# Modulation units emitted two by two in the first phase of a hybrid decoder step, with a fifth weight buffer

## The chip, the core and the metric

The kernel runs on one core of a Trainium2 chip. The metric is the device time of one execution in microseconds. The core has five engines that matter here: TensorE (PE, its weight loads PEld), VectorE (DVE), ScalarE (ACT), GpSimd (POOL) and SyncE (SP), whose queue issues nearly all DMA transfers, in order.

## What is computed

One inference step of a decoder layer with three token mixers, for 256 prompt tokens and 8 x 4 sample tokens, 288 rows in all. What matters here is how the layer begins: nine condition vectors (one for the prompt, eight for the samples) go through one large product, whose result modulates the normalised input, and the modulated input goes through the input projection.

```
def _layer(x, c, w_ada, b_ada, g_norm, w_in, ...):
    m = jax.nn.silu(c) @ w_ada + b_ada
    shift, scale, gate = jnp.split(m[:, None, :], 3, axis=-1)
    h = _rmsnorm(x, g_norm) * (1 + scale) + shift
    (u_a, v_a, z_a, qkv_b, z_b, a_b, b_b, q_c, k_c, v_c, z_c, qi_c, ki_c, wi_c) = _split_in(h @ w_in)
    ...
    mix = jnp.concatenate([y_a, y_b, y_c], axis=-1)
    x = x + gate * (mix @ w_out)
```

The model width is 4096, `w_ada` is 4096 x 12288, `w_in` 4096 x 14960, and all numbers are 32 bits wide. The mixers themselves, the final norm and the cache outputs come later in the kernel and are not touched.

## The kernel before

**Dense products.** A weight tile `w` holds 2 x 128 rows and 512 columns (512 KB). It is loaded by SyncE into one of `N_RAW` = 4 buffers and split, 128 rows at a time, into a high part `wh` (a cast on ACT) and the rest `wl` (a subtraction on DVE), with `N_SPLIT` = 4 buffers each. h is split in the same way into `hH` and `hL`. For each 128 columns and 128 rows there are three products of 288 columns (`wh` with `hH`, `wh` with `hL`, `wl` with `hH`), which add up in one of four accumulators `acc0` to `acc3`, each with one buffer. One `w` tile is thus 2 x 4 x 3 = 24 products.

**Modulation units.** The class `Ada` is one unit: two tiles `wa` of 128 x 1024 (512 KB each), and four small products of 32 x 512 that stand on four column groups of TensorE at once; since each is carried out in two passes, the trace shows eight records. The nine condition vectors are the fixed operand, padded to 32. Enough units after each other give shift and scale for 256 or 512 features, from which `make_h` builds h for these features.

**The first phase.** It is cut into 11 stages by features of h (`STEPS`: six stages of 256 features, then five of 512). In each stage the features' part of 12 column groups is computed: a narrow group `c` of 112 columns first, then eleven groups of 512. Each group ends with an addition on DVE (a copy on ACT in the first stage) that evicts the accumulators. The units of a stage must be done before its dense products. Stage 0 has 8 units, which run alone at the start. The other 120 are spread over the dense work of the stages before theirs.

**What sets the order.** The list of all units, dense and modulation, is made once, by the loop at line 899. `rate` is units per dense unit so that each later stage's units are done `LEAD` units ahead, and

```
            e = min(len(la), n0 + int(rate * (j + 1)) // PAIR * PAIR)
            W.units += [u] + la[n:e]
```

puts into the list as many modulation units as `rate` has made due, rounded down to a multiple of `PAIR`. Loads are then issued in the order of this list by `prefetch` as far as buffers are free: `w` into `N_RAW`, `wa` into `N_ADA`. All go through SyncE's queue, so a load that waits for its buffer holds up all that stand behind it. A `wa` buffer is free when the unit that read it is done. At the end of the first phase the pools are exchanged, and a second phase (attention, delta rule, further dense groups, output projection) runs with units of its own, which load into `w` buffers and are governed by other constants.

Of the kernel before, what the change touches and what calls it, by code (L numbers as in the profile page):

```python
# [36 lines left out]

GCOL = [512 * i for i in range(22)] + [C_QC + 512 * i for i in range(7)]
FULL = [(0, 128), (128, 128), (256, 128), (384, 128)]
N_RAW, N_ADA, N_SPLIT = 4, 4, 4  # L40
N_BANK = 4
HOP = 0.22
LEAD = 5
BACKLOG = 2.0
CALM = 2.5
NH = 3
LEAD0 = 0
GMO = 12
PAIR = 1
GATE = 8  # L50
GATE0 = 0
GPAIR = 1
# [328 lines left out]
def tile_hybrid_step(ctx: ExitStack, tc: tile.TileContext, I, O):  # L381
# [517 lines left out]
    while i < len(lb):  # L899
        rate, nxt = max([((min(len(la), la_end[j] + LEAD) - n) / (at_[j] - at_[i]), j) for j in range(i + 1, len(lb))],  # L900
                        default=(0, len(lb)))
        us = [u for x in lb[i:nxt] for u in x]
        n0 = n
        for j, u in enumerate(us):
            e = min(len(la), n0 + int(rate * (j + 1)) // PAIR * PAIR)
            W.units += [u] + la[n:e]
# [1576 lines left out]
```

## Time and profile before

| | |
|---|---|
| runs | 2639.38, 2645.76, 2648.55 us; median 2645.76 |
| profiled execution | 2644.57 us, span 2642.8 us |
| mean granted TensorE clock | 0.986 |
| busy | PE 96%, PEld 85%, DVE 62%, ACT 40%, POOL 19% |
| HBM | 587.54 MB read, 24.95 MB written |

The span runs from the first to the last instruction of the program; the execution's own time has 1.8 us around it. A busy share is the time in which an engine had at least one instruction under way. All durations below are from the profiled execution.

### The profile page before, as it was taken

The page shows a single profiled execution, that of the slowest core. Times are in us where ns is not written, and L with a number is a line of the kernel's source. Part 1 is how long each engine was busy: PE and PEld are TensorE (multiplying, and loading weights), DVE is VectorE, ACT ScalarE, POOL GpSimd, SP SyncE. Part 2 cuts the span into 40 slices and gives each one's busy share as a digit, 9 for nine tenths or more (in the row PEclk, how much of TensorE's full clock was granted, in tenths as well). Part 3 has the DMA queues.
Part 4 walks back from the last instruction along what each step waited for, and adds up shares of the span by engine and source line. Part 5 has one row for each costly group of instructions (what it writes and reads, how often), then busy time and mean ns, then how long its engine had stood idle before and what let it go on. Part 6 is the DMA issues. An engine that isn't in the chain of part 4 may idle for free.

```text
span 2642.8 us, 52171 instructions
## 1 busy us (share of the span) xinstructions
PE 2531.5 (96%) x19684; PEld 2237.9 (85%) x19684; DVE 1629.5 (62%) x3633; ACT 1064.3 (40%) x2440; POOL 495.5 (19%) x1137
## 2 busy tenths in 40 slices
PE   5999999999998999999999989999999999999997
PEld 2777878888897878877789969989989989999997
DVE  3377765555567777744457658568576667555554
ACT  3433233323244443334254444444444544444443
POOL 1000000000001042263542333443440210000000
PEclk9999999999999999999999999999999999999998
DMA  7998988888656477677767547567568465655564
GB/s 276 339 326 327 346 320 301 313 312 302 239 171 209 162 236 239 207 278 251 255 221 248 173 147 245 179 212 255 178 202 267 146 193 183 179 181 177 175 187 164
DMA packets 234964, 615.91 MB, mean 233 GB/s; under 512 B 38856, under 2 KB 92348, under 8 KB 234712
## 3 DMA queue, kind: packets, MB, share of 16 engines
q1 hardware_dynamic: 223672, 574.65, 64.6%
q0 software_dynamic: 11040, 37.92, 4.2%
q8 instruction: 155, 2.54, 0.4%
q14 instruction: 97, 0.79, 0.1%
HBM read 587.54 MB, written 24.95 MB: 232 GB/s over the span
## 4 chain that ended last, share of the span: by engine, by line
PE 85%; DMA 6%; DVE 3%; issue 2%; POOL 2%; ACT 1%; SPq 0%; another core or an unknown queue 0%; ACTq 0%; DVEq 0%; POOLq 0%
PE acc L74 68%; PE ada L74 7%; DMA kraw<-in_cache_k_dram,ixk 2%; DMA wa<-in_w_ada_t_dram 1%; PE Sup L74 1%; PE kT L74 1%; PE YP L74 1%; DVE wl L74 1%; DMA w<-in_w_in_t_dram 1%; PE v L74 1%; PE so L74 1%; PE gram L74 1%; PE o L74 1%; DMA prev<-in_state_conv_dram 0%; DMA vraw<-in_cache_v_dram,ixv 0%
## 5 line engine op out<-in xcount | busy, mean ns | idle before, releaser
L74 DVE TENSOR_TENSOR wl<-w,wh 128x512 fp32r<-128x512 f32 (+1 forms) x1216 | 803.0, 682 | 694.9 <-ACT wh L74 645.1
L74 ACT CAST wh<-w 128x512 fp32r<-128x512 f32 (+1 forms) x1216 | 714.3, 611 | 1173.3 <-PE acc L74 846.0
L74 PE MATMUL acc<-hH,wh 128*128 128x288 f32 (+1 forms) x3744 | 1159.7, 310 | 14.4 <-ACT hH L74 8.7
L74 PE MATMUL acc<-hH,wl 128*128 128x288 f32 (+1 forms) x3744 | 1108.7, 296 | 6.0 <-DVE wl L74 3.9
L74 PE MATMUL acc<-hL,wh 128*128 128x288 f32 (+1 forms) x3744 | 1107.8, 296 | 1.3 <-issue 0.9
L74 PEld LDWEIGHTS acc<-hH,wh 128*128 128x128 f32 (+1 forms) x3744 | 706.4, 189 | 175.6 <-ACT wh L74 90.2
L74 PEld LDWEIGHTS acc<-hH,wl 128*128 128x128 f32 (+1 forms) x3744 | 706.9, 189 | 9.7 <-DVE wl L74 7.6
L74 PEld LDWEIGHTS acc<-hL,wh 128*128 128x128 f32 (+1 forms) x3744 | 707.4, 189 | 4.4 <-issue 3.2
L74 PE MATMUL acc<-mL,wh 128*128 128x288 f32 x1024 | 302.4, 295 | 2.5 <-DVE mL L74 2.5
L74 PE MATMUL acc<-mH,wh 128*128 128x288 f32 x1024 | 304.3, 297 | 0.0
L74 PE MATMUL acc<-mH,wl 128*128 128x288 f32 x1024 | 302.8, 296 | 0.0
L74 PEld LDWEIGHTS acc<-mL,wh 128*128 128x128 f32 x1024 | 193.0, 188 | 2.7 <-DVE mL L74 2.7
L74 PEld LDWEIGHTS acc<-mH,wh 128*128 128x128 f32 x1024 | 192.9, 188 | 0.2
L74 PEld LDWEIGHTS acc<-mH,wl 128*128 128x128 f32 x1024 | 192.9, 188 | 0.0
L74 PE MATMUL ada<-wa,cT 128*32 128x512 f32 x1024 | 149.9, 619 | 17.6 <-DMA wa<-in_w_ada_t_dram 17.6
L74 DVE TENSOR_TENSOR zb<-zb,acc 128x288 f32<-128x288 f32 x160 | 70.6, 451 | 41.1 <-PE acc L74 40.4
L74 POOL TENSOR_TENSOR htmp<-yT,gaT 128x32 f32<-128x32 f32 x20 | 7.7, 387 | 449.9 <-DVE gaT L74 449.9
L74 POOL TENSOR_SCALAR frs<-frs 128x1 f32<-128x1 f32 (+1 forms) x3 | 0.9, 296 | 451.2 <-DVE frs L74 451.1
L74 POOL TENSOR_SCALAR tap<-xp,cwT 128x32 f32<-128x32 f32 x144 | 79.5, 552 | 0.1
L74 DVE TENSOR_TENSOR R<-R,R 128x248 f32<-128x248 f32 (+30 forms) x248 | 72.5, 292 | 10.8 <-DMA w<-in_w_in_t_dram 2.2
L74 DVE SCALAR_TENSOR_TENSOR cv<-xp,cwT,cv 128x256 f32<-128x256 f32 x144 | 70.3, 488 | 3.7
L74 POOL DMA_INDIRECT vraw<-in_cache_v_dram,ixv x64 | 65.2, 1019 | 31.2 <-issue 14.7
(462 smaller groups left out, 2350.5 us busy)
## 6 DMA issues: line engine op xcount, KB each, us to landing
w<-in_w_in_t_dram SPq DMA_DIRECT2D x464, 512.0 KB
wa<-in_w_ada_t_dram SPq DMA_DIRECT2D x256, 512.0 KB
w<-in_w_ada_t_dram SPq DMA_DIRECT2D x128, 512.0 KB
w<-in_w_out_t_dram SPq DMA_DIRECT2D x128, 512.0 KB
St<-in_state_dn_dram SPq DMA_DIRECT2D x16, 512.0 KB
out_dram<-St SPq DMA_DIRECT2D x16, 512.0 KB
X<-in_x_prompt_dram SPq DMA_DIRECT2D x8, 512.0 KB
XF<-in_x_prompt_dram SPq DMA_DIRECT2D x16, 256.0 KB
```

The source lines that it names most:

```text
L74: r = f(*a, **k)
```

## The change

Three constants.

```
-N_RAW, N_ADA, N_SPLIT = 4, 4, 4
+N_RAW, N_ADA, N_SPLIT = 4, 5, 4
 N_BANK = 4
 HOP = 0.22
-LEAD = 5
+LEAD = 6
...
-PAIR = 1
+PAIR = 2
```

With `PAIR` = 2 the modulation units come two at a time, `LEAD` = 6 makes the spread end one unit further ahead of each stage, and there are five `wa` buffers. No instruction is added or removed.

The first place is TensorE's queue at the start of the second stage, where the narrow group is followed by the first wide one. `ada` is the accumulator of the modulation units (x4 is one unit), `acc` with 112 columns the narrow group, with 128 a wide one. Before:

```order
L74 MATMUL ada<-wa,cT 32x512 x4
L74 MATMUL acc_1160<-hH_479,wh 112x288
L74 MATMUL acc_1160<-hL_491,wh 112x288
L74 MATMUL acc_1160<-hH_479,wl 112x288
L74 MATMUL acc_1160<-hH_479,wh 112x288
L74 MATMUL acc_1160<-hL_491,wh 112x288
L74 MATMUL acc_1160<-hH_479,wl 112x288
L74 MATMUL ada<-wa,cT 32x512 x4
L74 MATMUL acc_1178<-hH_479,wh 128x288
```

The same place after:

```order
L74 MATMUL ada<-wa,cT 32x512 x8
L74 MATMUL acc_1164<-hH_483,wh 112x288
L74 MATMUL acc_1164<-hL_495,wh 112x288
L74 MATMUL acc_1164<-hH_483,wl 112x288
L74 MATMUL acc_1164<-hH_483,wh 112x288
L74 MATMUL acc_1164<-hL_495,wh 112x288
L74 MATMUL acc_1164<-hH_483,wl 112x288
L74 MATMUL acc_1180<-hH_483,wh 128x288
```

Two units now stand together ahead of the narrow group, and none is left between it and the wide one. Of the eleven narrow groups six are followed at once by a unit in before and two after; the four that are no longer so are those of the first, second, sixth and tenth stage.

The second place is SyncE's queue in the second stage. `wa` are tiles of modulation units, `w` of dense products. Before:

```order
L74 DMA wa_1314<-in_w_ada_t_dram 128x1024
L74 DMA wa_1316<-in_w_ada_t_dram 128x1024
L74 DMA w_1318<-in_w_in_t_dram 128x1024
L74 DMA wa_1381<-in_w_ada_t_dram 128x1024
L74 DMA wa_1383<-in_w_ada_t_dram 128x1024
L74 DMA w_1389<-in_w_in_t_dram 128x1024
```

After:

```order
L74 DMA wa_1162<-in_w_ada_t_dram 128x1024
L74 DMA wa_1224<-in_w_ada_t_dram 128x1024
L74 DMA wa_1226<-in_w_ada_t_dram 128x1024
L74 DMA wa_1232<-in_w_ada_t_dram 128x1024
L74 DMA w_1234<-in_w_in_t_dram 128x1024
L74 DMA w_1236<-in_w_in_t_dram 128x1024
L74 DMA w_1256<-in_w_in_t_dram 128x1024
L74 DMA wa_1258<-in_w_ada_t_dram 128x1024
L74 DMA wa_1395<-in_w_ada_t_dram 128x1024
```

The four `wa` tiles of a pair now stand together, and two or three `w` tiles behind them. The first of the four (`wa_1162`, then `wa_1258`) has the fifth buffer and can go out ahead of the others, which stand in the queue until the pair before has run and freed their buffers. Between two pairs there are two blocks of 24 products, but a single one twice in the first stage; from the second to the sixth stage two and three in turn, up to the ninth three, and then four or five.

## Rows read from the trace of the kernel before

**Rows 1.** The page: busy time by engine; chain that ended last, by engine.

```profile
PE 2531.5 (96%) x19684; PEld 2237.9 (85%) x19684; DVE 1629.5 (62%) x3633; ACT 1064.3 (40%) x2440; POOL 495.5 (19%) x1137
...
PE 85%; DMA 6%; DVE 3%; issue 2%; POOL 2%; ACT 1%; SPq 0%; another core or an unknown queue 0%; ACTq 0%; DVEq 0%; POOLq 0%
```

**Rows 2.** Five stretches: busy by engine (PE to POOL), granted clock, DMA share, GB/s.

```profile
0.00:56.50 56.50, 28.17 (x150) 12.10 (x150) 19.33 (x46) 20.73 (x39) 13.15 (x36) 0.97 0.83 296
56.50:114.60 58.10, 56.92 (x379) 40.80 (x379) 17.67 (x33) 30.27 (x73) 1.88 (x8) 0.95 0.85 305
114.60:720.20 605.60, 602.71 (x4396) 491.26 (x4392) 377.80 (x792) 183.53 (x335) 19.86 (x64) 1.00 0.86 313
720.20:803.00 82.80, 76.76 (x548) 74.95 (x548) 58.30 (x123) 36.26 (x71) 2.38 (x9) 0.94 0.56 176
803.00:2642.80 1839.80, 1766.98 (x14221) 1618.80 (x14219) 1156.40 (x2639) 793.50 (x1925) 458.19 (x1020) 0.99 0.64 205
```

**Rows 3.** Waits of PE in the third stretch: us in total, times, longest.

```profile
PE acc L74 <- DVE v_c L74: 2.1, 4, 0.6
PE acc L74 <- ACT wh L74: 0.6, 1, 0.6
```

**Rows 4.** A stretch in which DMA is full, columns as in rows 2.

```profile
120.00:128.00 8.00, 8.00 (x55) 6.33 (x55) 4.95 (x12) 2.17 (x4) 0.00 (x0) 1.00 1.02 407
```

**Rows 5.** Timeline of PE around one lone unit: start, duration, operation.

```profile
299.82 0.29 PE L74 MATMUL acc<-hH,wl 128*128 128x288 f32 x1
300.04 1.07 PE L74 MATMUL ada<-wa,cT 128*32 128x512 f32 x8
301.04 0.40 PE L74 MATMUL acc<-hH,wh 128*128 128x288 f32 x1
301.28 0.30 PE L74 MATMUL acc<-hL,wh 128*128 128x288 f32 x1
...
304.20 0.29 PE L74 MATMUL acc<-hH,wl 128*128 128x288 f32 x1
```

**Rows 6.** Records of the units' products: ns min/median/max, first and last start.

```profile
L74 PE MATMUL ada<-wa,cT x1024: 592/616/1063, 20.0 to 720.7; 128*32 128x512 f32 x171
```

**Rows 7.** Timeline of PE at the start, units alone, idle time before in brackets.

```profile
20.02 3.11 PE L74 MATMUL ada<-wa,cT 128*32 128x512 f32 x8 [12.08 <-DMA wa<-in_w_ada_t_dram]
...
32.05 1.05 PE L74 MATMUL ada<-wa,cT 128*32 128x512 f32 x4 [0.34 <-DMA wa<-in_w_ada_t_dram]
...
42.39 4.87 PE L74 MATMUL ada<-wa,cT 128*32 128x512 f32 x16 [3.24 <-DMA wa<-in_w_ada_t_dram]
```

**Rows 8.** The chain that ended last, at the start: start, us, what.

```profile
26.01 6.00 DMA wa<-in_w_ada_t_dram
...
35.67 6.67 DMA wa<-in_w_ada_t_dram
```

**Rows 9.** The same chain in the first stage.

```profile
80.47 6.09 DMA wa<-in_w_ada_t_dram
...
86.61 1.05 PE ada L74 x4
```

**Rows 10.** Timeline of SyncE's issues behind the unit of rows 5.

```profile
301.14 0.81 SPq L74 DMA_DIRECT2D wa<-in_w_ada_t_dram  x2
```

**Rows 11.** Timeline of PE: end of a narrow group, no unit behind.

```profile
165.72 0.29 PE L74 MATMUL acc<-hH,wl 128*112 128x288 f32 x1
166.64 0.37 PE L74 MATMUL acc<-hH,wh 128*128 128x288 f32 x1 [0.64 <-DVE v_c L74]
```

**Rows 12.** Timeline of PE behind the first stage, units alone.

```profile
115.55 2.12 PE L74 MATMUL ada<-wa,cT 128*32 128x512 f32 x8
...
121.00 1.87 PE L74 MATMUL ada<-wa,cT 128*32 128x512 f32 x8
```

**Rows 13.** Timeline of PE: the last stage's first product.

```profile
727.10 0.58 PE L74 MATMUL acc<-hH,wh 128*112 128x288 f32 x1 [4.48 <-ACT hH L74]
```

**Rows 14.** Waits of ScalarE in the third stretch: us, times, longest.

```profile
ACT wh L74 <- DMA w<-in_w_in_t_dram: 103.1, 32, 5.4
```

## Prediction

> **What bounds the kernel now.** I read the page first, then the run cut into five stretches, then the waits inside the third of them, then single instructions. The page says that TensorE is busy for 96% of the span and that 85% of the chain that ended last is TensorE's own work [rows 1]. The five stretches [rows 2] are: up to the first dense product (56.5 us), the first stage with 13 interleaved modulation units (58.1 us), the stages with the other 107 (605.6 us), the last stage without units (82.8 us), and all that comes after (1839.8 us). The edit changes the first three alone: behind the last unit both programs have the same order. In the third stretch TensorE is busy for 602.7 of 605.6 us, and its waits there come to 2.7 us [rows 2, 3]. So time is saved there by giving TensorE less to do, and lost by making it wait. DMA moves 313 GB/s there at a share of 0.86; where it is full it moves 407 [rows 2, 4], which is 1.29 us for a 512 KB tile (524,288 B / 407 GB/s).
>
> **What a unit costs TensorE.** In a run of dense products one starts every 0.133 us (22 steps from 301.28 to 304.20) [rows 5]. Around a lone unit it goes: last product 299.82, unit 300.04, next product 301.04, the one after it 301.28. Two steps of 0.133 would do for what took 1.46, so the unit costs 1.19 us. Of this 0.09 is lost on entry (0.22 for 0.133), 0.11 on the second product after it (0.24 for 0.133), and some of the 1.00 in the middle on the way out. How much, I take from the unit's inside: its eight records are two passes on each of four column groups. One record lasts a median of 0.616 us by the profile's model [rows 6] and the unit 1.07 from first start to last end [rows 5], so the second pass starts 0.45 after the first; half a unit, two column groups alone, takes the same 1.05 [rows 7]. So passes follow each other at 0.45, and a unit that follows a unit would cost two of them, 0.906, in place of 1.19. **Each merge of two lone units saves 0.286 us.** No trace of before has two units back to back with their tiles there, so this is an estimate, between 0.09 (the entry alone is saved) and 0.33 (a pass takes 0.43). I take 0.286, since the pace of passes shows in every unit.
> The Trainium skill, TensorEngine Tiling (Array Packing), Key Properties, says that a change of tiling mode drains TensorE; its page TensorE: Matmul & The Clock Gate, Single matmul latency, puts the constant that a warm stream hides at 166 ns. Two of these a merge would be 0.33 us, and the merges below 17.9 us in place of 15.4; the row decides for the smaller.
>
> **The terms, in order of time.**
> *Start, -4.0.* The first 16 tiles come at the pace of release: the first unit starts at 20.02 and the last half unit at 46.2 (the run that starts at 42.39 lasts 4.87, its last half 1.05) [rows 7], 1.75 us a tile. The chain runs through tiles that were asked for only when a buffer came free (6.00 and 6.67 us) [rows 8]. Four tiles in a round trip of 7.0 us become five, 1.40 a tile; for the 11 tiles after the first five that is 3.9. What follows is a fixed chain (transposes, modulated h, first product) and moves with it. Bounds: 0, and 11 x (1.75 - 1.29) = 5.1.
> *First stage, +1.8.* A block is the 24 products of one w tile, 24 x 0.133 = 3.19 us. Ideal for before: 11 blocks + 0.8 for the narrow group + 13 x 1.19 = 51.4. It took 58.1: 6.7 lost, 2.9 of it at the lower clock (0.95 granted means a tenth of the stretch at 1.2 GHz) [rows 2], so 3.8 in waits, as on the tile of 6.09 us [rows 9]. After the change 14 units stand there in 7 pairs: 14 x 1.19 - 7 x 0.286 = 14.7 for 15.5, so -0.8. But two of the pairs follow the one before after a single block. A first tile lands 5.2 to 6.7 us after its issue (6.67 for one; 6.00 and 6.09 for two second tiles, which were issued 0.43 later and land 1.29 later) [rows 8 to 10]. SyncE issues 1.10 after a unit's start (301.14 against 300.04) [rows 5, 10]. So the last of the three tiles that a pair still needs lands at 1.10 + 5.2 + 2 x 1.29 = 8.9 from the start of the pair before. With one block between, it is used at 3.19 + 2.10 + 0.91 = 6.2: 2.7 late, twice, +5.4. The 3.8 of old waits go: with two blocks between, tiles are in time (below). And the unit between the first narrow group and the next covered a copy and a split of weights, of which about 1 us is now waited for. -0.8 + 5.4 - 3.8 + 1.0 = +1.8. Bounds -3 and +4.
> *One unit earlier, -1.2.* The first stage holds 14 units for 13, the later stretch 106 for 107.
> *Merges, -15.4.* 107 lone units become 53 pairs: 54 switches fewer, x 0.286. Bounds -4.9 and -17.8.
> *Narrow groups, +2.4.* After each stage's 112-column group the next group needs the same accumulator, which DVE must have evicted. A bare wait costs 0.64 idle, 0.79 in all (165.72 to 166.64 for a step of 0.13) [rows 11]; four of these make up the 2.1 us of the third stretch [rows 3]. A unit in between covers it. By the order of after, three later stages lose that cover: 3 x 0.79.
> *Late tiles, +3.6.* From the second to the sixth stage pairs follow each other after two and three blocks in turn. Two blocks: next pair at 2 x 3.19 + 2.10 = 8.5, its second unit at 9.4; its last tile lands at 8.9 with 5.2, at 10.4 with 6.7. I take 0.3 for each of 12 such gaps. With three blocks it is used at 12.6, never late. The w tiles issued behind them land from 10.2 on and are first used at 13.8, so 3.6 us cover ScalarE's and DVE's split of some 1.3; without that cover each gap would wait for it. Bounds 0 and 12 x 1.0 = 12.
> By the Trainium skill, DMA: Bandwidth & Descriptors, Anatomy of one DMA, a lone 512 KB transfer takes 2.0 + 524288/436e3 = 3.2 us (a fit made on GpSimd's path). By it no tile would be late after two blocks and the sum would be 3.6 lower; the transfers of these rows took longer, and I keep the rows.
> *Waits that go, -1.9.* Two units right behind the first stage took 2.12 and 1.87 where 1.07 is usual [rows 12]; their tiles now come in time.
> Sum: -4.0 + 1.8 - 1.2 - 15.4 + 2.4 + 3.6 - 1.9 = -14.7. The profiled execution took 2644.57 us (span 2642.8), 1.2 below the median of the three runs, 2645.76. **Predicted: 2644.57 - 14.7 = 2630 us.**
>
> The fifth buffer and the lead of six cost no engine anything: the same 256 tiles are loaded. The last stage starts right behind the last unit in both programs, so its wait of 4.48 us for h [rows 13] stays.
>
> **Rivals.**
> A. The bunches come late throughout and eat the gain. For it: four tiles are asked for within some 2 us behind a latency of 4 to 5, and DMA is at 0.86 already. With late tiles at 12, no gain at the start and the first stage at +4: -14.7 + 8.4 + 4.0 + 2.2 = -0.1, 2644. Against it: six or seven tiles have 8.5 and 11.7 us to come in, and take 7.7 and 9.0.
> B. Slower: SyncE's single queue. It issues in order, and will stand at a wa tile until a pair is done, with all later w tiles behind. ScalarE waits 103 us for w tiles already [rows 14]. If each two-block gap then ends in a restart that nothing hides (5.2 - 1.29 = 3.9), 12 of them cost 47: -14.7 - 3.6 + 47 = +29, 2673. It decides from 1.5 us a gap on (18.3 / 12). Against it: the 3.6 us by which w tiles are early in my ledger.
> C. A pair saves the entry alone: merges -4.9, sum -4.2, 2640. For it: no row has a pair. Against it: the passes' pace.
> D. What is gained up to the last unit is given back later. Against it: the part after is the same program, and its transfers are asked for from there. 2644.
>
> **How the numbers follow.** A measurement of this kernel can tell about 0.3%, 8 us, from no change. Forecast 0.72, with its own range 2618 (all good bounds: -5.1 - 3 - 1.2 - 17.8 + 2.4 - 1.9 = -26.6) to 2637; C 0.06; A 0.10; D 0.04; B 0.08. Faster by over 0.3%: the forecast, 0.72. Within it: A, C and D, 0.20. Slower: B, 0.08. The range of 8 in 10 leaves out B, the far half of A and D, and a little of the good end: 2618 to 2643.
>
> **What would show it.** Right: pairs of 1.98 us (1.07 + 0.906), with the next product 1.90 after the start; the third stretch shorter by 12 to 15 us; the first product at 52 to 53. Wrong: TensorE idle before units on DMA wa up to the sixth stage (A), products waiting for the split of w in every gap (B), pairs of 2.1 or more (C), or a part after the last stage that is longer than 1840 us (D).

## The result, and the profile after

| | before | after |
|---|---|---|
| median | 2645.76 us | 2630.81 us |
| lowest to highest (5 runs each) | 2639.38 to 2648.55 | 2626.0 to 2633.52 |
| profiled execution, span | 2644.57, 2642.8 | 2626.0, 2624.3 |

The ratio is 0.9941, with a 95% interval of 0.9921 to 0.9961: 15 us faster by the medians, 18.5 by the two profiled executions (the profiled execution of after is the fastest of its five runs). The page of after, against [rows 1]:

```profile
PE 2509.4 (96%) x19684; PEld 2245.5 (86%) x19684; DVE 1625.4 (62%) x3633; ACT 1065.7 (41%) x2440; POOL 496.1 (19%) x1137
...
PE 85%; DMA 7%; DVE 3%; POOL 2%; issue 2%; ACT 1%; SPq 0%; ACTq 0%; DVEq 0%; POOLq 0%
```

TensorE has the same number of instructions and 22 us less busy time. The five stretches, cut at the same events as [rows 2]:

```profile
0.00:52.00 52.00, 26.26 (x151) 12.08 (x151) 19.39 (x47) 20.75 (x39) 13.18 (x36) 1.00 0.91 341
52.00:111.50 59.50, 56.65 (x386) 41.74 (x386) 17.63 (x33) 30.43 (x73) 1.89 (x8) 0.94 0.79 302
111.50:703.20 591.70, 583.21 (x4382) 495.36 (x4380) 373.55 (x792) 183.17 (x335) 19.98 (x64) 1.00 0.86 318
703.20:789.50 86.30, 80.27 (x570) 77.86 (x570) 59.85 (x126) 37.82 (x75) 2.36 (x9) 0.94 0.56 174
789.50:2624.30 1834.80, 1763.05 (x14207) 1618.42 (x14205) 1155.00 (x2637) 793.55 (x1922) 458.68 (x1020) 0.98 0.64 205
```

The start is 4.5 us shorter, the first stage 1.4 longer, the third stretch (up to the last pair) 13.9 shorter; the two last rows are cut a little apart from those of before and are compared below by one event. In the third stretch TensorE is busy 19.5 us less, but idle 8.5 us where it was idle 2.9. Around one pair:

```profile
549.03 0.29 PE L74 MATMUL acc<-hH,wl 128*128 128x288 f32 x1
549.25 1.93 PE L74 MATMUL ada<-wa,cT 128*32 128x512 f32 x16
551.11 0.40 PE L74 MATMUL acc<-hH,wh 128*128 128x288 f32 x1
551.34 0.30 PE L74 MATMUL acc<-hL,wh 128*128 128x288 f32 x1
```

Against [rows 5]: from the product before to the second product behind it are 2.31 us for two steps of 0.133, so a pair costs 2.05 where two lone units cost 2 x 1.19. The medians say the same to the third decimal: from the product before to the product behind, 107 lone units (in before) took 1.221 and 53 pairs 2.079 us, so the second unit adds 0.858 where a lone one costs 1.19, and a merge saves 0.335 us, not 0.286. TensorE's waits in the third stretch, against [rows 3]:

```profile
PE acc L74 <- DVE v_c L74: 6.7, 6, 1.4
PE acc L74 <- ACT wh L74: 1.7, 1, 1.7
```

These are the waits behind narrow groups. One of them, with ACT and DVE (lines of other work left out):

```profile
440.67 0.39 PE L74 MATMUL acc<-hH,wh 128*112 128x288 f32 x1
...
441.23 1.14 ACT L74 CAST wh<-w 128x512 fp32r<-128x512 f32 x2 [2.15 <-PE acc L74]
...
441.88 1.29 DVE L74 TENSOR_TENSOR wl<-w,wh 128x512 fp32r<-128x512 f32 x2 [2.13 <-ACT wh L74]
...
442.23 0.29 PE L74 MATMUL acc<-hH,wl 128*112 128x288 f32 x1
...
443.09 0.45 DVE L74 TENSOR_TENSOR v_c<-v_c,acc 112x288 f32<-112x288 f32 x1
443.68 0.37 PE L74 MATMUL acc<-hH,wh 128*128 128x288 f32 x1 [1.16 <-DVE v_c L74]
```

Read it from ACT: its cast for the wide group waits for TensorE ([2.15 <-PE acc]) and starts at 441.23, once the narrow group's first products have run. Only then is a split buffer free: the four pieces of the narrow group hold all four. DVE's two splits (1.29) follow, and `v_c` stands behind them. The step from 442.23 to 443.68 is 1.45 us where a product follows a product in 0.133; in [rows 11] it was 0.92. In the stages of 512 features before had a lone unit in the middle of the narrow group, and its 1.19 us let DVE finish the splits ahead of `v_c`. The corresponding stage of before:

```profile
451.52 1.07 PE L74 MATMUL ada<-wa,cT 128*32 128x512 f32 x8
451.75 1.29 DVE L74 TENSOR_TENSOR wl<-w,wh 128x512 fp32r<-128x512 f32 x2 [1.28 <-ACT wh L74]
...
453.60 0.45 DVE L74 TENSOR_TENSOR v_c<-v_c,acc 112x288 f32<-112x288 f32 x1 [0.56 <-PE acc L74]
...
454.20 0.37 PE L74 MATMUL acc<-hH,wh 128*128 128x288 f32 x1 [0.64 <-DVE v_c L74]
```

The longest of these waits has another cause. In the third stage ACT's cast waits for the load of the w tile, not for a split buffer:

```profile
159.84 2.39 ACT L74 CAST wh<-w 128x512 fp32r<-128x512 f32 x4 [5.12 <-DMA w<-in_w_in_t_dram]
...
162.30 0.37 PE L74 MATMUL acc<-hH,wh 128*128 128x288 f32 x1 [1.74 <-ACT wh L74]
```

The late pairs are in the first stage, where one block stands between two pairs (PE and SyncE's queue):

```profile
60.42 1.92 PE L74 MATMUL ada<-wa,cT 128*32 128x512 f32 x16
...
61.51 1.28 SPq L74 DMA_DIRECT2D wa<-in_w_ada_t_dram  x3
...
65.67 2.27 PE L74 MATMUL ada<-wa,cT 128*32 128x512 f32 x12
...
69.04 1.05 PE L74 MATMUL ada<-wa,cT 128*32 128x512 f32 x4 [1.11 <-DMA wa<-in_w_ada_t_dram]
```

The three open tiles are issued 1.09 after the pair before started, and the last half unit, which a pair with its tiles in hand begins about 0.9 after the pair's start, begins 3.37 after it. This pair was 2.5 us late, a second one (99.62) 1.6, and three later ones (254.22, 295.02, 315.05) 0.61, 0.70 and 0.92.

### The profile page after: what moved, and what is told of

Its sections match the earlier page's. It is cut to its first block, busy times and chain, and to the rows that moved or that the text cites. A ratio compares the mean times of both kernels' runs of the same rounds, so it can differ in the third digit from the quotient of the medians.

```text
span 2624.3 us, 52262 instructions
## 1 busy us (share of the span) xinstructions
PE 2509.4 (96%) x19684; PEld 2245.5 (86%) x19684; DVE 1625.4 (62%) x3633; ACT 1065.7 (41%) x2440; POOL 496.1 (19%) x1137
## 4 chain that ended last, share of the span: by engine, by line
PE 85%; DMA 7%; DVE 3%; POOL 2%; issue 2%; ACT 1%; SPq 0%; ACTq 0%; DVEq 0%; POOLq 0%
PE acc L74 68%; PE ada L74 7%; DMA kraw<-in_cache_k_dram,ixk 2%; DMA wa<-in_w_ada_t_dram 1%; DMA vraw<-in_cache_v_dram,ixv 1%; PE kT L74 1%; DMA w<-in_w_in_t_dram 1%; PE Sup L74 1%; DVE wl L74 1%; PE YP L74 1%; PE v L74 1%; PE gram L74 1%; PE o L74 1%; POOL vraw L74 1%; PE S L74 1%
## 5 line engine op out<-in xcount | busy, mean ns | idle before, releaser
L74 PE MATMUL ada<-wa,cT 128*32 128x512 f32 x1024 | 135.7, 605 | 15.8 <-DMA wa<-in_w_ada_t_dram 15.5
L74 PEld LDWEIGHTS ada<-wa,cT 128*32 128x32 f32 x1024 | 28.2, 109 | 72.9 <-issue 54.7
```

Source lines behind the costliest of these rows:

```text
L74: r = f(*a, **k)
```

## The experiments

All are the changed kernel with the edit shown. A ratio is to runs of the kernel before on the same chip, whose medians were 2644.8 to 2648.5. Stage times are from the traces: *start* ends with the first dense product, *first stage* with the first product of the second stage's narrow group, *stages 2 to 10* with that of the last stage's (so the wait of some 4.5 us for h is in it).

| kernel | median us | ratio to before | start | first stage | stages 2 to 10 |
|---|---|---|---|---|---|
| before | 2645.76 | | 56.53 | 58.04 | 612.53 |
| after: 5 buffers, pairs | 2630.81 | 0.9941 [0.9921, 0.9961] | 51.98 | 59.54 | 599.40 |
| 5 buffers, lone | 2638.45 | 0.9965 [0.9951, 0.9979] | 53.67 | 55.64 | 608.53 |
| 4 buffers, pairs | 2653.45 | 1.0020 [1.0008, 1.0032] | 55.77 | 66.66 | 610.09 |
| pair behind each narrow group | 2645.12 | 1.0002 [0.9991, 1.0014] | 52.72 | 55.17 | 616.27 |
| narrow group in third accumulator | 2625.63 | 0.9927 [0.9907, 0.9946] | 50.17 | 60.36 | 593.89 |
| own split buffers | 2626.0 | 0.9928 [0.9902, 0.9954] | 54.17 | 60.74 | 595.48 |
| both of these | 2626.1 | 0.9924 [0.9902, 0.9947] | 53.92 | 61.54 | 594.40 |
| both, lone units | 2630.35 | 0.9941 [0.9922, 0.9961] | 51.19 | 56.53 | 605.36 |
| 6 buffers, pairs | 2619.85 | 0.9901 [0.9878, 0.9923] | 50.97 | 56.42 | 595.10 |
| 6 buffers, third accumulator | 2615.76 | 0.9886 [0.9867, 0.9904] | 50.28 | 57.26 | 590.77 |
| the same, lone units | 2625.11 | 0.9926 [0.9910, 0.9942] | 50.24 | 53.53 | 604.16 |
| the same, three together | 2607.91 | 0.9867 [0.9846, 0.9889] | 51.31 | 59.54 | 583.29 |
| the same, lone in the first stage | 2606.97 | 0.9867 [0.9833, 0.9900] | 49.88 | 56.08 | 582.00 |

From the last stage's first product to the end it is 1910 to 1920 us in all of these, with no order in it (before 1915.7, after 1913.4). The stage times are of one profile each. The granted clock of the first stage lies between 0.92 and 0.97 in them; an estimate of what it costs, (1 - clock) x stage, goes from 1.7 us (lone in the first stage) to 4.8 (third accumulator), so differences of up to 3 us between first stages can be the clock's. The start of the seven kernels with five buffers, the same work in all, took 50.2 to 54.2 us.

**One half alone: the fifth buffer.**

```
-LEAD = 6
+LEAD = 5
-PAIR = 2
+PAIR = 1
```

> The changed kernel with PAIR 1 and LEAD 5 as before, so the fifth buffer alone. Theory (the traces of both kernels: the buffer is worth the 4.5 us by which the first product comes earlier and some late tiles in the first stage; the 107 units stay lone at 1.19 us each): first product at 52, third stretch about as long as before (602 to 607 us), 2637 to 2641 us, that is 6 to 11 slower than the changed kernel. Rival (the buffer is the whole gain, pairs give nothing net): 2631, equal to the changed kernel.

Measured: 2638.45, as the theory has it, though the first product comes at 53.67 and not at 52. Half of the gain is the buffer's: the first stage is 2.4 us shorter than before, stages 2 to 10 are 4.0 shorter. Of these 4.0, 2.2 are lone units that no longer come late (in before 2.9 us behind the first stage, among them those of [rows 12]; here 0.7); the other 1.8 are shorter waits between dense products.

**The other half: pairs with four buffers.**

```
-N_RAW, N_ADA, N_SPLIT = 4, 5, 4
+N_RAW, N_ADA, N_SPLIT = 4, 4, 4
```

> The changed kernel with four buffers: pairs and LEAD 6, but all four tiles of a pair are asked for only when the pair before has run. Theory (a pair's last tile lands one transfer, 1.29 us, later than with five; after two blocks it is used 9.4 us after the pair before and lands at 10.2 to 11.7): first product back at 56.5 (+4.5), two one-block gaps of the first stage +1.3 each, 0.8 to 2.3 late in each of some 12 two-block gaps (+10 to +28); 2645 to 2665 us, at or above the kernel before. Rival (the lead of the loads suffices, only the start is lost): 2635.

Measured: 2653.45, slower than before. Pairs and buffer are not worth together what they are worth apart: by the medians on the same chip +7 and -8 alone, -15 together. Two pairs of the first stage come 4.0 and 3.5 us late, a third 0.5, eleven later ones 0.1 to 2.7. And w tiles come late behind some of them (SyncE's queue, ACT and PE):

```profile
92.56 1.92 SPq L74 DMA_DIRECT2D wa<-in_w_ada_t_dram  x4
...
94.52 1.53 SPq L74 DMA_DIRECT2D w<-in_w_in_t_dram  x2
95.02 1.14 ACT L74 CAST wh<-w 128x512 fp32r<-128x512 f32 x2 [3.05 <-DMA w<-in_w_in_t_dram]
...
95.69 0.40 PE L74 MATMUL acc<-hH,wh 128*128 128x288 f32 x1 [1.79 <-ACT wh L74]
```

This is rival B's mechanism, in single places.

**A pair behind each narrow group, to cover its waits.**

```
-            e = min(len(la), n0 + int(rate * (j + 1)) // PAIR * PAIR)
+            if len(u.tiles) == 1:
+                e = n
+                if j + 1 == len(us) or len(us[j + 1].tiles) > 1:
+                    e = max(n, min(len(la), n0 + int(rate * (j + 1) + 1.4) // PAIR * PAIR))
+            else:
+                e = max(n, min(len(la), n0 + int(rate * (j + 1)) // PAIR * PAIR))
```

> The changed kernel with pairs shifted so that one stands right behind each narrow group of the stages that have units, between its products and the next group's. The number of pairs and blocks is the same. Theory (a pair of 1.9 us covers the eviction and the split): the idle time of 8.4 us in the third stretch behind narrow groups and the 1.0 us of the first stage go, at most 2 us come back as late tiles: 7 to 10 us faster than the changed kernel, 2621 to 2624. Rival (the unevenness makes tiles late by as much, or the waits show up elsewhere): 2629 to 2632.

Measured: 2645.12. The theory fell, and by the edit's own doing: in the second stage and those of 512 features the shifted pair follows the one before with nothing but the narrow group between them (629.37 and 633.00 below). The waits for `v_c` did go, but nine pairs come 20.6 us late in all (0.6 to 4.4 each), and behind seven of them the products wait another 1.4 for w (SyncE's queue, PE and ACT):

```profile
629.37 1.93 PE L74 MATMUL ada<-wa,cT 128*32 128x512 f32 x16
...
630.46 1.28 SPq L74 DMA_DIRECT2D wa<-in_w_ada_t_dram  x3
631.79 8.83 SPq L74 DMA_DIRECT2D w<-in_w_in_t_dram  x5
633.00 1.05 PE L74 MATMUL ada<-wa,cT 128*32 128x512 f32 x4
...
637.00 1.05 PE L74 MATMUL ada<-wa,cT 128*32 128x512 f32 x4 [0.24 <-DMA wa<-in_w_ada_t_dram]
638.32 2.42 ACT L74 CAST wh<-w 128x512 fp32r<-128x512 f32 x4 [8.69 <-DMA w<-in_w_in_t_dram]
...
638.99 0.40 PE L74 MATMUL acc<-hH,wh 128*128 128x288 f32 x1 [0.94 <-ACT wh L74]
```

What it shows is the price of short gaps: the kernel is some 14 us slower than the changed one, as much as the change had gained.

**The narrow group in another accumulator.**

```
-                self.st.acc[j] = acc_tile(j)
+                self.st.acc[j] = acc_tile(2 if m == 112 else j)
```

> The changed kernel, with the narrow group of 112 columns in the third accumulator in place of the first, so that the wide group behind it does not need the accumulator that DVE is to evict. Theory (in the trace of the changed kernel TensorE idles 6.7 us in six waits for v_c behind narrow groups; the eviction is late because the splits of the next w tile stand ahead of it on DVE, and nothing else holds the products): these waits go, 5 to 7 us faster than the changed kernel, 2624 to 2626. Rival (the products behind are held by the split weights as well, which come no earlier): the idle time moves from v_c to wl or wh, 2630 to 2632.

Measured: 2625.63; stages 2 to 10 are 5.5 us shorter. No wait for `v_c` is left, but some of its time is found again as waits for split weights:

```profile
PE acc L74 <- ACT wh L74: 1.8, 3, 1.0
PE acc L74 <- DVE wl L74: 1.5, 4, 0.9
```

**Split buffers of their own for the narrow group.**

```
...
-            self.wh = W.tile(wpool, list(w.shape), F32R, "wh", "wh", N_SPLIT)
-            self.wl = W.tile(wpool, list(w.shape), F32R, "wl", "wl", N_SPLIT)
+            pool, own = (pools["p1"][1], "n") if self.small else (wpool, "")
+            self.wh = W.tile(pool, list(w.shape), F32R, "wh" + own, "wh", N_SPLIT)
+            self.wl = W.tile(pool, list(w.shape), F32R, "wl" + own, "wl", N_SPLIT)
```

(`small` is true for the narrow group, whose pieces then no longer count in the limit of four.)

> The changed kernel with buffers of their own for the split weights of the narrow group. Theory (the narrow group's pieces hold all four split buffers, so the wide group's casts start only when its first products have run, and its two splits of 1.29 us stand ahead of the addition v_c on DVE): the splits are made earlier, DVE takes v_c at once, and the waits of 1.3 to 1.9 us behind narrow groups fall to the bare 0.8: 3 to 4 us faster than the changed kernel, 2627 to 2628. Rival (the splits come late because the w tiles do): 2630 to 2632.

Measured: 2626.0. The splits of the same place (DVE and PE) are now made ahead of the narrow group, and the wait is the bare one of [rows 11]:

```profile
438.24 1.29 DVE L74 TENSOR_TENSOR wl<-w,wh 128x512 fp32r<-128x512 f32 x2
...
442.28 0.46 DVE L74 TENSOR_TENSOR v_c<-v_c,acc 112x288 f32<-112x288 f32 x1 [2.39 <-PE acc L74]
...
442.88 0.37 PE L74 MATMUL acc<-hH,wh 128*128 128x288 f32 x1 [0.64 <-DVE v_c L74]
```

All seven steps behind bare narrow groups in stages 2 to 10 are now 0.93 us; after had one of 0.93, four of 1.46, one of 1.71 and one of 2.03. So the split buffers made the difference between 0.93 and 1.46. The step of 2.03 does not count for this: it was the late w tile of the third stage, and with six buffers and shared split buffers it is 0.93 too.

**Both.**

> Own split buffers for the narrow group and the third accumulator for it, both. Theory (with the third accumulator alone some 4 us of waits for wl and wh behind narrow groups were left in the third stretch; they go as the splits come earlier): 3 to 4 us faster than with the accumulator alone, 2621 to 2623. Rival (what is left there is late w tiles): 2625 to 2627.

Measured: 2626.1, the rival's number. Most of what is left is late w tiles, and the trace says why (SyncE's queue, ACT, PE): four `wa` issues stand for 5.54 us until buffers are free, the next `w` is issued behind them, and ACT has waited 11.23 us for w:

```profile
442.35 5.54 SPq L74 DMA_DIRECT2D wa<-in_w_ada_t_dram  x4
445.02 1.92 PE L74 MATMUL ada<-wa,cT 128*32 128x512 f32 x16
447.99 0.38 SPq L74 DMA_DIRECT2D w<-in_w_in_t_dram  x1
448.35 1.90 ACT L74 CAST wh<-w 128x512 fp32r<-128x512 f32 x3 [11.23 <-DMA w<-in_w_in_t_dram]
...
449.02 0.40 PE L74 MATMUL acc<-hH,wh 128*128 128x288 f32 x1 [2.07 <-ACT wh L74]
```

**The same with lone units.** (`PAIR = 1`, `LEAD = 5`)

> As the kernel with both (own split buffers, third accumulator), but PAIR 1 and LEAD 5: lone units with five buffers, where no narrow group waits in either. It prices the pairs by themselves. Theory (54 merges of 0.335 us are 18.1; against it some 6 us of late pairs): 11 to 13 us slower than the kernel with both, 2633 to 2636. Rival (a merge is worth my 0.286, or the late pairs eat more): 5 to 9 slower, 2627 to 2631.

Measured: 2630.35, 4 slower than with pairs: nearer to the rival. Pairs win 11.0 us in stages 2 to 10 and give 5.0 back in the first stage (61.54 for 56.53), which the theory had counted too low; some 1.5 of the 5.0 can be the clock's (0.93 for 0.95).

**A sixth buffer.**

```
-N_RAW, N_ADA, N_SPLIT = 4, 5, 4
+N_RAW, N_ADA, N_SPLIT = 4, 6, 4
-        triS = tl("p1", [P, P], "triS")
+        triS = tl("xp", [P, P], "triS")
```

> The changed kernel with a sixth weight buffer for the units (a mask tile of 0.5 KB moves to another pool to make room). Theory (a pair is late where its third open tile lands behind the use; with six buffers two of its four tiles go out ahead and the last lands one transfer, 1.29 us, earlier): the 4.1 us of late pairs in the first stage fall to about 1.5, the 2.3 us in the later stages go, the start gains up to 1; 4 to 6 us faster than the changed kernel, 2625 to 2627. Rival (SyncE's queue stands in order anyway, and the w tiles behind lose what the wa tiles gain): 2630 to 2633.

Measured: 2619.85, 11 us faster than after by the medians, 8.5 by the profiles: the first stage is 3.1 shorter, stages 2 to 10 are 4.3 shorter. Late pairs are down from 6.4 us to 0.8, and none is left behind the first stage. That is one transfer's lead, as the theory had it. The whole is more than it had priced: another 2.0 us of the 4.3 are shorter waits between dense products, 1.1 of them the late w tile of the third stage, which is in time here.

**Six buffers and the third accumulator.** (both edits above)

> Six buffers and the third accumulator for the narrow group. Theory (with six buffers late pairs are gone, and 8 us of waits behind narrow groups are what is left in the third stretch; with the third accumulator, as with five buffers, 5 to 6 of them go): 5 to 6 us faster than six buffers alone, 2614 to 2615. Rival (the waits move to the w tiles that stand in SyncE's queue): 2618 to 2620.

Measured: 2615.76, 4.1 faster than six buffers alone: between the two. The `v_c` waits go, some of their time stays as waits for wl.

**The same with lone units.** (`PAIR = 1`, `LEAD = 5`)

> As the kernel with six buffers and the third accumulator, but PAIR 1 and LEAD 5: lone units, with tiles in time and narrow groups that hold nothing up in either. It prices the merges alone. Theory (0.335 us each, 54 of them in the stages behind the first and 6 in the first): the third stretch 17 to 18 us longer than with pairs, the first stage 2 us shorter or alike; 2630 to 2633. Rival (0.286 each, as I had it): 15 us longer, 2628 to 2630.

Measured: 2625.11, 9.3 us slower than the pairs. Stages 2 to 10 are 13.4 longer, less than either number, because pairs still bring waits in the dense products: over all steps from product to product, except those right behind a unit, what exceeds 0.133 sums up to 5.94 us with pairs and 0.69 with lone units. Without that the difference is 18.6, of which 1.2 is one unit more, counted with its own entry and exit; that leaves 17.5 for the 53 merges of 106 units, 0.33 us each.

**Three together.** (`PAIR = 3`, `LEAD = 7`)

> As the kernel with six buffers and the third accumulator, but PAIR 3 and LEAD 7: three units together, all six of their tiles asked for when the three before have run. Theory (20 switches fewer than with pairs are worth 6.7 us; the last of six tiles lands at 1.1 + 5.2 + 5 x 1.29 = 12.8 us and is used at 14.0 after three blocks, at 10.9 after two, twice in the first stage): 2 to 4 us late there, little elsewhere, 3 to 5 us faster than with pairs. Rival (six tiles behind each other hold the w tiles back in SyncE's queue, and products wait for them): 5 us or more slower than with pairs.

Measured: 2607.91, 7.9 faster than pairs by the medians, more than the theory's 3 to 5; stages 2 to 10 are 7.5 shorter, the first stage 2.3 longer. The third unit adds what the second added:

```profile
569.28 0.29 PE L74 MATMUL acc<-hH,wl 128*128 128x288 f32 x1
569.51 2.78 PE L74 MATMUL ada<-wa,cT 128*32 128x512 f32 x24
572.22 0.40 PE L74 MATMUL acc<-hH,wh 128*128 128x288 f32 x1
```

1.07, 1.93 and 2.78 us for one, two and three, so 0.86 for each one that follows.

**Three together, but lone units in the first stage.**

```
-            e = min(len(la), n0 + int(rate * (j + 1)) // PAIR * PAIR)
+            e = min(len(la), n0 + int(rate * (j + 1)) // (PAIR if i else 1) * (PAIR if i else 1))
```

> As the kernel with three units together, but lone units in the first stage, where 15 units stand in 11 blocks and bunches follow each other after one to two blocks. Theory (what bunches lose there are late tiles of gaps that are too short: the first stage took 59.5 us with threes and 53.5 with 13 lone units; 15 lone ones need 55.9): first stage 55 to 57, 3 to 4 us faster than threes throughout, 2604 to 2605. Rival (the first stage is held by its w tiles, whatever the order of the units): first stage 59 to 60, 2608.

Measured: the first stage takes 56.08 us, 3.5 shorter, as the theory had it. With threes two bunches there were 4.2 us late in all; here none is. So short gaps are what bunches lose there, but the 3.5 is not all theirs: the granted clock was 0.97 for 0.94, some 1.7 us, and against it stand the merges that are given up. In the median of the whole (2606.97) it is 0.9 less, and the two ratios are equal: the total does not show it. These two versions beat the changed kernel by some 23 us by the medians, 20 by the ratios.

## Why the prediction held, term by term

**Start, -4.0: measured -4.5**, and that buffers set it is shown: over all profiles the first product comes at 56.2 on average with four buffers (2 of them), at 52.5 with five (7, from 50.2 to 54.2) and at 50.5 with six (5). So five are worth 3.6 on average; the 4.5 of the one pair of profiles can be in part chance (the granted clock of the start was 0.97 before and 1.00 after).

**First stage, +1.8: measured +1.5.** Both late pairs are where the text put them, 4.1 us for the 5.4 it summed; the wait behind the first narrow group is 1.3 for the 1.0; the older waits that go are 3.7 for 3.8, of which 2.0 stood at 83.76, where before already had two units in a row with a tile late. With -0.8 for merges and the unit more these add up to 0.9 of the 1.5. That short gaps are the cause is shown by the sixth buffer, with which the 4.1 fall to 0.8, and by the lone units in the first stage.

**One unit earlier and merges, -1.2 and -15.4: by the measured costs -1.2 and -17.8.** Here a size was off. The step was to take the pace of two passes inside a lone unit, 0.45, for the pace between units. In the pair of 549.25 the second unit's first pass starts 0.429 after the first unit's second, its own second 0.430 later, and the unit adds 0.858 in all; 0.454 is the step from the first to the second pass behind dense products alone. The estimate lay at 0.286, its bound at 0.33 with a pass of 0.43; the profile after has 0.335, the comparison of six-buffer kernels 0.33. And the prediction counted one merge too many: 106 units in 53 pairs are 53 merges, since the unit that moves away takes its entry and exit with it, in the -1.2. By the Trainium skill, TensorE: Matmul & The Clock Gate, Single matmul latency, a warm matmul has a constant of 166 ns (stated for one bf16 matmul; these products are of 32 bits); two of these a merge, the prediction's estimate from that page, make 0.33, and the measured size agrees with it. That it is this constant which a merge saves was not tried by itself.

**Narrow groups, +2.4: measured +6.2** (the excess of all dense steps in stages 2 to 10, without those behind units or with other work of TensorE between, is 6.19 us before and 12.44 after). This step failed. The prediction priced the three groups that lose the unit behind them at the bare wait of [rows 11], 0.79 each, and put the four groups that were bare already at nothing. The three took 0.80, 1.57 and 1.33. Of the four, the three in the stages of 512 features became 0.53 longer each, and the one in the third stage 1.1. In the stages of 512 features of before a unit inside the narrow group had covered the splits; without it `v_c` waits behind 1.29 us of them. The own split buffers, with which these steps are back at the bare wait, show this cause for them; the third accumulator shows that the waits are worth 5.5 us on the path. The 1.1 of the third stage is the late w tile shown above. (The four bare waits of before are three for `v_c` and the one for wh of [rows 3], 2.6 us in all; the 2.1 that the text took for them holds another, shorter wait.)

**Late tiles and waits that go, +3.6 - 1.9: measured -0.6.** Late pairs behind the first stage come to 2.3 us, nearly all at three places, where before had 2.9 of late units and waits behind them. In the other two-block gaps the tiles were in time, as with the 5.2 us that the text had as one end. That margin is thin: with one buffer less it is gone.

**The sum.** Stages 2 to 10 were forecast at -12.5 and took -13.1 (the terms as measured sum to -13.4), by errors against each other (2.4 us of merges and 2.3 of tiles to the good, 3.8 of narrow groups to the bad). So the mechanisms of the gain were right, but that the sum comes within 1 us is luck. The profiles differ by 2.3 us more, behind the last stage's first product; that part varies by 10 us among profiles of these kernels and tells nothing. The forecast of 2630, reckoned from the profiled execution of before, meets the median, 2630.81; the profiled execution of after, 2626.0, lies 4 below it. Rival C (the entry alone) is out by the pairs' 1.93; rivals A and B describe what four buffers and the shifted pairs did; in this change they show in single places only (five late pairs, one late w tile); D does not show.

## What to carry to other kernels

Count for each bunch of work how many of its tiles can be asked for before the bunch ahead has run: here one of four was enough to turn +7 us into -15, and two of four gave another 11 by the medians. A gap between bunches must be longer than issue, latency and the transfers still open, or every tile behind them in the same queue is late too. And before a filler is moved, look at all that it covers where it stands: one inside a group may cover a split and an eviction, one ahead of it neither.

## What the runs showed of the hardware

Units of four column groups follow each other at 0.86 us, while a lone one between dense products costs 1.19: entry and exit cost 0.335 us together, and this holds for two and for three in a row. The granted clock of the first stage was 0.92 to 0.97, and not by the waits in it: 0.93 with 1.2 us of TensorE's waits (six buffers), 0.97 with 1.4 (five buffers, lone). The low part lies at its beginning, behind a start in which TensorE was idle for about half of the time (25.7 of 52.0 us in after): from 52.0 to 58.9 us after was granted 0.51, about 1.2 GHz, and from there to the end of the stage 1.00, 2.4 GHz. How long the low part lasts differs from profile to profile. The end of the kernel, which the edits touch little or not at all, varied by 10 us from profile to profile.
